# A hybrid decoder layer on one core: four small projection blocks moved from the first column tiles to the seventh, attention's units two ticks earlier, and one group's third weight sum made by accumulating transfers

## The chip, the cores and the metric

The kernel runs on one core of a Trainium2 chip. The metric is device time in microseconds (us) of one execution. TensorE (PE) multiplies; VectorE (DVE), ScalarE (ACT) and GpSimd (POOL) do the element-wise work; SP and POOL issue the DMAs that this change is about.

## The reference

One decoder layer over 512 tokens and 2048 columns, in fp32. `z = rms_norm(x) @ w_in` is cut by columns into q, k, v, an attention gate, and four parts of a convolution branch. Attention is causal over a window of 128 keys, with 16 query heads on 4 key heads, a norm and a partial rotation of q and k, and a learned sink. The convolution branch is `c_b * conv3(c_c * c_h)`, with three taps. Each branch is gated by a SiLU, and `x = x + concat(...) @ w_out`. Then

```
gate = sigmoid(rms_norm(x) @ w_ple_gate + b_ple_gate)
e    = rms_norm(p @ w_ple_proj)
x    = x + gate * e
```

where p is 512 x 256. The change touches where `p @ w_ple_proj` is computed, the timing of attention, and how a sum of weight blocks for `w_ple_gate` is made.

## The kernel before, in words

Every fp32 product is made of three matmuls on rounded halves: `halves` (L198) casts a tile to its high part on ACT (wh, L199) and subtracts on DVE for the low part (wl, L200). A matmul takes a 128 x 128 weight and 512 columns.

**The grouped products.** Most of the work is nine groups (five of `w_mid`, which are columns of w_in, two of `w_out`, two of `w_ple_gate`) of 28 steps, 12 matmuls each, in a scheme with seven products f = 1 to 7 over sums of weight blocks. `loads` and `load_more` (L144) bring blocks of 512 KB into the buffers wx, wy and ws; `sums` makes the sums of blocks in place. The third of them, for f = 7, is `tt(x, y, x, subtract)` on DVE (L191), four per group. For the groups in T3_BY_DMA that subtraction is left out, and L1368 to L1372 queue something else for each of the four blocks: `load_again` (L171) loads one block anew over the x block, and three steps later `add_block` (L166) adds another to it by an accumulating DMA that POOL issues. The first goes out after step 3 + 2i of the group (5 + 2i in the groups 5 and 7, which LATE lists), i counting the blocks. The order of PE is as written in the code in all parts; in the groups that of the other engines is too.

**The section before and the section here.** Group 0 runs first. Then (L670 on) comes the section that the change is about, where only PE's order is by hand and a scheduler orders the rest of the engines. It has seven column tiles of w_in, c_c and c_h of four convolution channels' tiles in turn, the last c_h behind the loop at L1383. `gemm_tile` (L702) makes a tile: 16 k, three matmuls each (L711), two weight blocks of 512 KB from a list `jobs`. `next_job` takes the next block of the list, splits the one after it, and `fetch` loads two further ahead into four raw buffers (L619). After each odd k it calls `tick`: eight ticks a tile, six matmuls apart. `at(when, fn)` hangs work on a tick. Attention and the preparation of k and q ride on these ticks:

- tick 4: `make_k(1)`, tick 6: `make_v`, tick 7: `make_k(0)`. `make_k` turns k on PE into a psm bank, of which there is one (ps_m), copies it to kr on ACT (L740), and makes khh and kll, high and low halves, by four more ACT casts (L745, L746) and four DVE subtractions (L747, L748).
- the norm and rotation of half of q (`square_q`, `rstd_q`, `rope_q`) at ticks 18 to 26.
- 16 units of attention `attention(j, n, when)`, with when = 13 + 35u // 15 for unit u: `turn_q` for every second unit at when − 4 (PE turns q into the same psm bank, L772; ACT and DVE make st, L776 and L777), `scores` at when (eight matmuls, L794 and L795, into two pss banks; the mask and row maximum on DVE, L800, into a prob buffer, of which there are two; exponentials on ACT, L807), `turn` at when + 5 (PE turns prob into pst, L822; halves give pth and ptl), `values` at when + 8 (into one pso bank, L832), and an accumulating DMA at when + 12.

**e's blocks.** `e_block(n)` (L854) makes one of four column blocks of p @ w_ple_proj for all 512 tokens: 24 matmuls (L874) into four banks, two pss and two pst, those that scores and turn use, each drained by a Square on ACT with its row sums (L865), a product by the gain on DVE (L867), and a DMA that POOL issues (L868). It takes one job of the list. `mids` says before which k of which tile an e block runs: block 0 at k = 8 of the first tile, blocks 1, 2, 3 at k = 0, 4, 8 of the second. The four w_ple_proj blocks stand among the first eight jobs.

**The first gate group** is group 7. Its gate values get their bias by accumulating DMAs on POOL (`add_b`, L1266), then a sigmoid (L1285), and a product with e (L1289).

Of the kernel before, what the change touches and what calls it, by code (L numbers as in the profile page):

```python
# [27 lines left out]
TQ, TK, TV, TGA, TCB, TCC, TCH, TGC = 0, 8, 10, 12, 20, 28, 36, 44  # L28
# [7 lines left out]
def hymba_layer(ctx: ExitStack, tc: tile.TileContext, io):  # L36
# [57 lines left out]
    NG = len(groups)  # L94
    chunks = [(0, 1, 2, 3)] * 5 + [(0, 1, 3, 2), (0, 1, 2, 3), (0, 1, 3, 2), (0, 1, 3, 2)]
    LATE = (5, 7)
    T1_BY_DMA, T3_BY_DMA = (0, *range(2, NG - 1)), (4, 5, 6)
    steps = []
    for g in range(NG):
        c0, c1, c2, c3 = chunks[g]  # L100
# [23 lines left out]
    for g in range(NG):  # L124
        w, n = groups[g]
# [72 lines left out]
    def halves(h, l, src):  # L198
        nc.scalar.copy(h, src)  # L199
        tt(l, src, f32(h), op=ALU.subtract)  # L200
# [259 lines left out]
    def flat(t):  # L460
        return t.rearrange("p a b -> p (a b)")
# [32 lines left out]
    for c in range(8):  # L494
# [20 lines left out]
        for i in range(2):  # L515
            k = 2 * c + i
# [47 lines left out]
    def head_sums(z, out, junk):  # L564

        sq = junk.rearrange("p (h d) -> p h d", d=HD)
        nc.scalar.activation(sq, z, AF.Square)
        nc.vector.tensor_reduce(out, sq, axis=mybir.AxisListType.X, op=ALU.add)

    def head_rstd(ms, eps):  # L570


        stt(ms, ms, 1.0 / HD, eps.unsqueeze(2).broadcast_to(ms.shape), op0=ALU.mult, op1=ALU.add)
        power(ms, ms)
# [8 lines left out]
    def q_of(t, n):  # L583
        return qs[t, n].rearrange("p b (h d) -> p b h d", d=HD)
# [3 lines left out]
    def square_q(t, n, b, junk):  # L588
        if b == 0:
            rq[t, n] = small.tile([P, 2, 8], F32, name="msq", bufs=4)  # L590
        head_sums(q_of(t, n)[:, b], rq[t, n][:, b], junk("sqq"))

    def rstd_q(t, n):
        blocks = slice(2 * t, 2 * t + 2)
        head_rstd(rq[t, n], eps_tok[:, blocks])

    def rope_q(t, n):
        rope(q_of(t, n), 0, slice(2 * t, 2 * t + 2), mtile)
# [5 lines left out]
    for j, s in enumerate((6, 6, 7, 7, 9, 9, 10, 10)):  # L604
        soon(after, s, form7, j)

    jobs = [io["w_in"][TCC, 0], io["w_ple_proj"][0], io["w_in"][TCC, 1], io["w_ple_proj"][1],
            io["w_in"][TCH, 0], io["w_ple_proj"][2], io["w_ple_proj"][3], io["w_in"][TCH, 1]]
    for i in range(1, 4):
        jobs += [io["w_in"][t + i, c] for t in (TCC, TCH) for c in range(2)]  # L610
    raws, splits, job = {}, {}, [0]

    def blocks_of(t):
# [68 lines left out]
    def mtile(name):  # L682
        return misc.tile([P, T], F32, tag="m", name=name)
# [5 lines left out]
    def at(when, fn):  # L689
        later.append((when, len(later), fn))  # L690
# [31 lines left out]
    for t in range(2):  # L722
        rope_q(t, 1)
        for b in range(2):
            at(18 + 2 * t + b, lambda t=t, b=b: square_q(t, 0, b, mtile))
        at(20 + 2 * t, lambda t=t: rstd_q(t, 0))
        at(24 + 2 * t, lambda t=t: rope_q(t, 0))
    mask = cw.tile([P, 2 * P], F32, name="mask", bufs=1)
    nc.gpsimd.dma_start(mask, io["mask"])
    vv = vvp.tile([P, NB, NKV, 2, HD], F32R, name="vv")  # L730
# [51 lines left out]
    def attention(j, n, when):  # L782

        lo = 0 if n else P
        cell = {}

        def scores():
            sc = [ps_s.tile([P, 2, 2 * P], F32, name="pss") for _ in range(2)]
            ks = slice(n * P + lo - P, (n + 1) * P)
            for r in range(4):  # L790
                i = 2 * (n % 2) + r // 2
                q = turned[j, n // 2, r % 2][:, i * P : (i + 1) * P]
                out = sc[r // 2][:, r % 2, lo:]
                nc.tensor.matmul(out, q, khh[j][:, ks], start=True, stop=False)  # L794
                nc.tensor.matmul(out, q, kll[j][:, ks], start=False, stop=True)  # L795
            t = ap.tile([P, 4, 2 * P], F32, name="prob")
            negm, sums, sk = (small.tile([P, 4], F32, name=x) for x in ("negm", "sums", "sk"))
            r_q = rq[n // 2, j // 2][:, n % 2, 4 * (j % 2) : 4 * (j % 2) + 4]
            for r in range(4):
                nc.vector.tensor_tensor_reduce(  # L800
                    t[:, r, lo:], sc[r // 2][:, r % 2, lo:], mask[:, lo:], HD**-0.5, NEG,
                    ALU.add, ALU.max, negm[:, r : r + 1],
                )
            tt(negm, negm, r_q, op=ALU.mult)
            stt(negm, negm, -1.0, nsink[:, 4 * j : 4 * j + 4], op0=ALU.mult, op1=ALU.min)
            for r in range(4):
                nc.scalar.activation(  # L807
                    t[:, r, lo:], t[:, r, lo:], AF.Exp, scale=r_q[:, r : r + 1], bias=negm[:, r : r + 1],
                    accum_out=sums[:, r : r + 1],
                )  # L810
            tt(sk, sink[:, 4 * j : 4 * j + 4], negm, op=ALU.add)
            nc.scalar.activation(sk, sk, AF.Exp)
            tt(sums, sums, sk, op=ALU.add)
            nc.vector.reciprocal(rs[:, n, 4 * j : 4 * j + 4], sums)
            cell["t"] = t

        def turn():
            cell["pt"] = []
            for kt in range(lo // P, 2):
                pt_ = ps_t.tile([P, T], F32, name="pst")  # L820
                for r in range(4):
                    nc.tensor.transpose(pt_[:, r * P : (r + 1) * P], cell["t"][:, r, kt * P : (kt + 1) * P], ident)  # L822
                h, l = (ap.tile([P, T], F32R, name=x) for x in ("pth", "ptl"))
                halves(h, l, pt_)
                cell["pt"].append((n - 1 + kt, h, l))

        def values():
            po = ps_o.tile([P, 4, P], F32, name="pso")
            pts = cell["pt"]
            for i, (b, h, l) in enumerate(pts):  # L830
                w = vv[:, b, j].rearrange("p s d -> p (s d)")
                nc.tensor.matmul(po, w, h, start=i == 0, stop=False)  # L832
                nc.tensor.matmul(po, w, l, start=False, stop=i == len(pts) - 1)
            up = mtile("up").rearrange("p (r t) -> p r t", t=P)
            nc.scalar.copy(up, po)
            rows = attn_dram[j].rearrange("(r d) (n t) -> d r n t", d=HD, n=NB)[:, :, n]
            nc.gpsimd.dma_start(rows, up[:HD])
            cell["add"] = lambda: nc.gpsimd.dma_start(rows, up[HD:], accum_op=ALU.add)

        if n % 2 == 0:  # L840
            at(when - 4, lambda: turn_q(j, n // 2))
        at(when, scores)
        at(when + 5, turn)
        at(when + 8, values)
        at(when + 12, lambda: cell["add"]())

# [7 lines left out]
    def e_block(n):  # L854

        pg = pgs[n]
        if n < 3:
            load_pg(n + 1)
        ws = next_job()
        banks = [flat(ps_s.tile([P, 2, 2 * P], F32, name="pss")) for _ in range(2)]  # L860
        banks += [ps_t.tile([P, T], F32, name="pst") for _ in range(2)]

        def take_e(t):
            e = mtile("e")
            nc.scalar.activation(e, banks[t], AF.Square, accum_out=esq[:, t, n : n + 1])  # L865
            e = mtile("e")
            tt(e, banks[t], pg, op=ALU.mult)  # L867
            nc.gpsimd.dma_start(e_dram[t // 2][n][:, t % 2], e)  # L868

        for t in range(NB):  # L870
            for k in range(2):
                h, l = (a[:, k, t * P : (t + 1) * P] for a in pts)
                for i, (a, w) in enumerate(((h, ws[0]), (l, ws[0]), (h, ws[1]))):
                    nc.tensor.matmul(banks[t], a, w[:, k], start=k == 0 and i == 0, stop=k == 1 and i == 2)  # L874
            for i in (t,):
                take_e(i)
# [1 line left out]
    load_pg(0)  # L878
    order = [(j, n) for j in (2, 3, 0, 1) for n in range(NB)]
    for u, (j, n) in enumerate(order):  # L880
        attention(j, n, 13 + 35 * u // 15)
    mids = {0: {8: lambda: e_block(0)}, 1: {k: lambda n=n: e_block(n) for n, k in ((1, 0), (2, 4), (3, 8))}}


    for i in range(4):
        ps = gemm_tile(ps_g.tile([P, T], F32, name="psg"), mids.get(2 * i))
        zc = mtile("zc") if i < 3 else rowp.tile([P, T], F32, tag="rows", name="zc")
        tt(zc, ps, rx2, op=ALU.mult)
        if i == 3:
            break  # L890
        ps = gemm_tile(ps_g.tile([P, T], F32, name="psg"), mids.get(2 * i + 1))
        u = cw.tile([P, T + HD], F32, name="u")
        nc.gpsimd.memset(u[:, 0:2], 0.0)
        tt(u[:, 2 : T + 2], ps, zc, op=ALU.mult)
        y = mtile("yconv")
        nc.scalar.activation(y, u[:, 0:T], AF.Copy, scale=convw[:, 0, i : i + 1])
        for s in (1, 2):
            stt(y, u[:, s : s + T], convw[:, s, i : i + 1], y, op0=ALU.mult, op1=ALU.add)
        nc.gpsimd.dma_start(conv_dram[i], y)
# [493 lines left out]
    u, y = itile("u"), rowp.tile([P, T], F32, tag="rows", name="yconv")  # L1393
# [121 lines left out]
```

## Time and profile before

| what | us |
|---|---|
| median of 3 runs | 919.99 (919.91 to 920.25) |
| the profiled execution | 919.36 |
| its span | 917.6 |
| outside the span | 1.76 |
| PE busy | 905.9 |
| DVE busy | 723.8 |
| ACT busy | 542.7 |
| POOL busy | 160.8 |

The profile is of one execution. Start times are us from the span's start; the busy time of an instruction overlaps its neighbours', so two instructions that follow at once start a little closer than the first one's duration. In brackets behind a row stands how long the engine was idle before it, and what ended that. "X <- Y" in the list of waits reads: this instruction of X, waiting for that tile written by Y, in us in total, how many times, and the longest one. In a group of transfers the last number is the median time from issue to landing. A psum bank is named by its tile: psg the gemm's, psm, pss, pst, pso as above, psp the groups'.

### The profile page before, as it was taken

The page shows a single profiled execution, that of the slowest core. Times are in us where ns is not written, and L with a number is a line of the kernel's source. Part 1 is how long each engine was busy: PE and PEld are TensorE (multiplying, and loading weights), DVE is VectorE, ACT ScalarE, POOL GpSimd, SP SyncE. Part 2 cuts the span into 40 slices and gives each one's busy share as a digit, 9 for nine tenths or more (in the row PEclk, how much of TensorE's full clock was granted, in tenths as well). Part 3 has the DMA queues.
Part 4 walks back from the last instruction along what each step waited for, and adds up shares of the span by engine and source line. Part 5 has one row for each costly group of instructions (what it writes and reads, how often), then busy time and mean ns, then how long its engine had stood idle before and what let it go on. Part 6 is the DMA issues. An engine that isn't in the chain of part 4 may idle for free.

```text
span 917.6 us, 12067 instructions
## 1 busy us (share of the span) xinstructions
PE 905.9 (99%) x4178; PEld 751.4 (82%) x4178; DVE 723.8 (79%) x1063; ACT 542.7 (59%) x878; POOL 160.8 (18%) x211
## 2 busy tenths in 40 slices
PE   9999999999999999999999999999999999999997
PEld 8888888878888888888888888888888888887885
DVE  6878888788765777877768678987858887889678
ACT  6767847778863443454345357766556666555453
POOL 4232132143230001100120110102120111001100
PEclk9999999999999999999999999999999999999999
DMA  9999558434469767558578887858996993588647
GB/s 315 362 292 308 197 63 309 162 81 108 93 116 313 269 204 234 159 169 233 157 185 240 239 222 233 253 141 229 341 291 193 211 295 92 139 248 267 183 138 218
DMA packets 71389, 195.06 MB, mean 213 GB/s; under 512 B 8355, under 2 KB 14819, under 8 KB 71328
## 3 DMA queue, kind: packets, MB, share of 16 engines
q1 hardware_dynamic: 48096, 132.14, 42.3%
q0 software_dynamic: 23088, 62.15, 30.5%
q8 instruction: 32, 0.52, 0.2%
q14 instruction: 29, 0.24, 0.1%
q10 hardware_dynamic: 144, 0.01, 0.0%
HBM read 162.81 MB, written 31.46 MB: 212 GB/s over the span
## 4 chain that ended last, share of the span: by engine, by line
PE 89%; DVE 6%; ACT 3%; issue 2%; DVEq 0%; ACTq 0%
PE psp L241 67%; PE psg L711 6%; PE psp L519 5%; PE pst L241 4%; PE pst L993 2%; ACT prob L807 1%; PE pss L874 1%; PE pst L1391 1%; PE pst L874 1%; PE pst L822 1%; DVE wl L200 1%; DVE z L1289 1%; DVE prob L800 1%; DVE ptl L200 1%; PE pso L832 1%
## 5 line engine op out<-in xcount | busy, mean ns | idle before, releaser
L241 PE MATMUL psp<-wh,form 128*128 128x512 f32 x1280 | 395.3, 390 | 0.0
L241 PEld LDWEIGHTS psp<-wh,form 128*128 128x128 f32 x1280 | 239.4, 188 | 49.2
L241 PE MATMUL psp<-wl,form 128*128 128x512 f32 x640 | 249.5, 390 | 1.3 <-DVE wl L200 1.2
L200 DVE TENSOR_TENSOR wl<-wy,wh 128x1024 fp32r<-128x1024 f32 x108 | 131.5, 1222 | 60.3 <-ACT wh L199 59.7
L199 ACT CAST wh<-wy 128x1024 fp32r<-128x1024 f32 x108 | 113.4, 1051 | 90.2 <-PE psp L241 70.6
L241 PEld LDWEIGHTS psp<-wl,form 128*128 128x128 f32 x640 | 120.1, 188 | 27.4 <-DVE wl L200 2.5
L200 DVE TENSOR_TENSOR wl<-wx,wh 128x1024 fp32r<-128x1024 f32 x72 | 88.0, 1223 | 50.0 <-ACT wh L199 49.8
L199 ACT CAST wh<-ws 128x1024 fp32r<-128x1024 f32 x72 | 75.9, 1054 | 74.5 <-PE psp L241 53.8
L199 ACT CAST wh<-wx 128x1024 fp32r<-128x1024 f32 x72 | 75.6, 1052 | 74.3 <-PE psp L241 52.7
L241 PE MATMUL psp<-wh,hsh 128*128 128x512 f32 x304 | 118.6, 390 | 0.0
L241 PE MATMUL psp<-wl,hsh 128*128 128x512 f32 x304 | 118.3, 389 | 0.0
L241 PE MATMUL psp<-wh,hsl 128*128 128x512 f32 x304 | 118.3, 389 | 0.0
L200 DVE TENSOR_TENSOR wl<-ws,wh 128x1024 fp32r<-128x1024 f32 x72 | 88.1, 1223 | 27.1 <-ACT wh L199 26.8
L189 DVE TENSOR_TENSOR wy<-wy,ws 128x1024 f32<-128x1024 f32 x72 | 87.7, 1218 | 0.0
L241 PEld LDWEIGHTS psp<-wh,hsh 128*128 128x128 f32 x304 | 57.1, 188 | 11.8
L241 PEld LDWEIGHTS psp<-wh,hsl 128*128 128x128 f32 x304 | 57.1, 188 | 11.8
L241 PEld LDWEIGHTS psp<-wl,hsh 128*128 128x128 f32 x304 | 57.1, 188 | 11.8
L711 PE MATMUL psg<-hsh,wh 128*128 128x512 f32 x112 | 45.2, 403 | 0.0
L711 PE MATMUL psg<-hsh,wl 128*128 128x512 f32 x112 | 43.8, 391 | 0.0
L711 PE MATMUL psg<-hsl,wh 128*128 128x512 f32 x112 | 43.8, 391 | 0.0
L199 ACT CAST wh<-raw 128x1024 fp32r<-128x1024 f32 (+1 forms) x29 | 29.2, 1006 | 22.5 <-DMA raw<-in_w_ple_proj 7.7
L200 DVE TENSOR_TENSOR wl<-raw,wh 128x1024 fp32r<-128x1024 f32 (+1 forms) x29 | 33.8, 1165 | 9.5 <-ACT wh L199 9.2
(218 smaller groups left out, 1307.1 us busy)
## 6 DMA issues: line engine op xcount, KB each, us to landing
ws<-in_w_mid SPq DMA_DIRECT2D x40, 512.0 KB, 4.5
wx<-in_w_mid SPq DMA_DIRECT2D x24, 512.0 KB, 4.2
wy<-in_w_mid SPq DMA_DIRECT2D x20, 512.0 KB, 7.6
h<-form POOLq DMA_DIRECT2D x32, 256.0 KB, 5.8
wy<-in_w_mid POOLq DMA_DIRECT2D x16, 512.0 KB, 8.1
raw<-in_w_in SPq DMA_DIRECT2D x16, 512.0 KB, 4.1
wx<-in_w_out SPq DMA_DIRECT2D x16, 512.0 KB, 7.6
ws<-in_w_out SPq DMA_DIRECT2D x16, 512.0 KB, 5.6
```

Source lines behind the costliest of these rows:

```text
L189: tt(y, y, got[g, "s1" if f == 6 else "s0", c], op=ALU.add)
L199: nc.scalar.copy(h, src)
L200: tt(l, src, f32(h), op=ALU.subtract)
L241: nc.tensor.matmul(ps[t], a, w[:, i], start=start and first and i == 0 and n == 0, stop=last and i == 1 and n == 2, skip_group_check=not s ...
L519: nc.tensor.matmul(kv_ps[t // 2][:, t % 2], hs[k][a][:, t * P : (t + 1) * P], kv_split[c][w][:, i], start=k == 0 and n == 0, stop=k == KT ...
L711: nc.tensor.matmul(ps, w[:, k % 8], a, start=k == 0 and n == 0, stop=k == KT - 1 and n == 2)
L800: nc.vector.tensor_tensor_reduce(t[:, r, lo:], sc[r // 2][:, r % 2, lo:], mask[:, lo:], HD**-0.5, NEG, ALU.add, ALU.max, negm[:, r : r + 1],)
L807: nc.scalar.activation(t[:, r, lo:], t[:, r, lo:], AF.Exp, scale=r_q[:, r : r + 1], bias=negm[:, r : r + 1], accum_out=sums[:, r : r + 1],)
L822: nc.tensor.transpose(pt_[:, r * P : (r + 1) * P], cell["t"][:, r, kt * P : (kt + 1) * P], ident)
L832: nc.tensor.matmul(po, w, h, start=i == 0, stop=False)
L874: nc.tensor.matmul(banks[t], a, w[:, k], start=k == 0 and i == 0, stop=k == 1 and i == 2)
L993: nc.tensor.transpose(pt[:, b], quads[b // 2][:, b % 2, f * P : (f + 1) * P], ident)
```

## The change

Three things are done.

1. The list of jobs holds the sixteen blocks of w_in in the order of the tiles, with the four blocks of w_ple_proj from the fourteenth place on (one before the seventh tile's second w_in block and three behind it). The e blocks 0, 1, 2 run at k = 8, 10 and 12 of the seventh tile, block 3 behind that tile and its product by rx2.
2. Attention's when is 11 + 35u // 15, so all units run two ticks earlier, and the first turn_q falls on tick 7. The turn comes at when + 6. The norm and rotation of q are three ticks earlier.
3. Group 7 is added to T3_BY_DMA: four DVE subtractions go, and four loads on SP and four accumulating DMAs on POOL, of 512 KB each, come in after the steps 5, 7, 9, 11 and three steps later.

```diff
-    T1_BY_DMA, T3_BY_DMA = (0, *range(2, NG - 1)), (4, 5, 6)
+    T1_BY_DMA, T3_BY_DMA = (0, *range(2, NG - 1)), (4, 5, 6, 7)
...
-    jobs = [io["w_in"][TCC, 0], io["w_ple_proj"][0], io["w_in"][TCC, 1], io["w_ple_proj"][1],
-            io["w_in"][TCH, 0], io["w_ple_proj"][2], io["w_ple_proj"][3], io["w_in"][TCH, 1]]
-    for i in range(1, 4):
-        jobs += [io["w_in"][t + i, c] for t in (TCC, TCH) for c in range(2)]
+    jobs = [io["w_in"][t + i, c] for i in range(4) for t in (TCC, TCH) for c in range(2)]
+    jobs[13:14] = [io["w_ple_proj"][0], jobs[13]] + [io["w_ple_proj"][i] for i in range(1, 4)]
...
-            at(18 + 2 * t + b, lambda t=t, b=b: square_q(t, 0, b, mtile))
-        at(20 + 2 * t, lambda t=t: rstd_q(t, 0))
-        at(24 + 2 * t, lambda t=t: rope_q(t, 0))
+            at(15 + 2 * t + b, lambda t=t, b=b: square_q(t, 0, b, mtile))
+        at(17 + 2 * t, lambda t=t: rstd_q(t, 0))
+        at(21 + 2 * t, lambda t=t: rope_q(t, 0))
...
-        at(when + 5, turn)
+        at(when + 6, turn)
...
-        attention(j, n, 13 + 35 * u // 15)
-    mids = {0: {8: lambda: e_block(0)}, 1: {k: lambda n=n: e_block(n) for n, k in ((1, 0), (2, 4), (3, 8))}}
+        attention(j, n, 11 + 35 * u // 15)
+    mids = {6: {k: lambda n=n: e_block(n) for n, k in ((0, 8), (1, 10), (2, 12))}}
...
         if i == 3:
+            e_block(3)
             break
```

The lines behind L610 stand two lower in the changed kernel, and the last ones one.

## The prediction

> **What bounds the kernel now.** I read the page first: the engines' busy time, and the chain that ended last.
>
> ```profile
> span 917.6 us, 12067 instructions
> PE 905.9 (99%) x4178; PEld 751.4 (82%) x4178; DVE 723.8 (79%) x1063; ACT 542.7 (59%) x878; POOL 160.8 (18%) x211
> ```
>
> TensorE (PE) works in 905.9 of 917.6 us. None of the edits adds or removes a matmul (4178 before, and none of the moved blocks changes its product), so the time can only move by what PE waits: 917.6 − 905.9 = 11.7 us. Second came PE's waits by releaser, third the windows, which say where the idle time lies (columns: the window, its length, then busy time of PE, PE's weight loads, DVE, ACT and POOL, the granted clock, the DMA share, GB/s).
>
> ```profile
> PE pst L822 <- DVE ptl L200: 2.4, 3, 1.5
> PE psp L241 <- DVE wl L200: 1.2, 1, 1.2
> PE pst L368 <- DVE zeros L364: 1.1, 1, 1.1
> PE pst L822 <- DVE negm L804: 0.6, 1, 0.6
> 126.00:150.00 24.00, 24.00 (x111) 19.89 (x110) 20.04 (x42) 15.95 (x30) 2.21 (x4) 1.00 0.79 219
> 165.50:274.00 108.50, 105.38 (x590) 89.14 (x589) 84.11 (x291) 84.24 (x222) 34.71 (x39) 1.00 0.47 107
> 274.00:286.00 12.00, 12.00 (x55) 9.93 (x54) 2.55 (x3) 2.91 (x4) 2.06 (x3) 1.00 0.87 253
> 817.00:828.00 11.00, 9.74 (x42) 7.43 (x41) 9.73 (x11) 7.44 (x9) 1.70 (x2) 1.00 0.81 234
> 905.00:917.60 12.60, 6.50 (x29) 5.07 (x27) 8.63 (x15) 2.25 (x5) 0.00 (x0) 0.88 0.80 261
> ```
>
> The change can reach two of these. In attention (165.5 to 274) PE idles 108.5 − 105.38 = 3.12 us. In the first gate group (817 to 828) it idles 11 − 9.74 = 1.26 us. The start (1.1) and the tail (6.1) are untouched. So the change can gain at most 3.12 + 1.26 = 4.4 us. The stretch from 126 to 150, where two e blocks stand now, has no wait at all: whatever goes wrong there is new time.
>
> The profiled execution took 919.36 us (917.6 of span, 1.76 around it), 0.63 below the median of 919.99. The sum is made against 919.36, and 0.63 is added at the end. The bound of 0.2%, about what a measurement of this kernel can tell from no change, is 1.84 us.
>
> **First part: e's blocks leave the first two column tiles.** The chain of waits gives PE's own order where they stand:
>
> ```profile
> 126.34 5.45 PE psg L711 x24
> 131.78 0.44 PE psm L739 x4
> 132.22 2.75 PE pss L874 x12
> 134.98 2.72 PE pst L874 x12
> 137.70 4.08 PE psg L711 x18
> 141.78 0.44 PE psm L739 x4
> ```
>
> Between the two L739 groups (the transposes of make_k(1) and make_k(0), at ticks 4 and 7) lie an e block, 2.75 + 2.72 = 5.47 us, and three ticks of the gemm, 4.08 us. The e block goes, the three ticks stay. Both groups write the one psm bank, so the second must wait until ScalarE (ACT) has read the first into kr. Now ACT's timeline (start, duration, and in brackets the idle time ahead and what ended it), with two transfers by time to landing ahead of it and one row of DVE behind it, used further down:
>
> ```profile
> rows_r<-rx_tok POOLq DMA_DIRECT2D x1, 2.0 KB, 11.3
> mask<-in_mask POOLq DMA_DIRECT2D x1, 128.0 KB, 12.8
> 127.10 1.02 ACT L320 ACTIVATE z<-psp 128x1024 f32<-128x1024 f32 x1
> 135.80 1.05 ACT L199 CAST wh<-raw 128x1024 fp32r<-128x1024 f32 x1 [7.67 <-DMA raw<-in_w_ple_proj]
> 136.75 0.68 ACT L740 ACTIVATE kr<-psm,kq 128x512 f32<-128x512 f32 x1
> 137.47 0.62 ACT L745 CAST khh<-kr 64x512 fp32r<-64x512 f32 x1
> 139.92 0.59 ACT L865 ACTIVATE e<-pss 128x512 f32<-128x512 f32 x1
> 163.90 0.69 DVE L867 TENSOR_TENSOR e<-pss,pg 128x512 f32<-128x512 f32 x1 [0.61 <-ACT e L865]
> ```
>
> ACT's first kr was ready to run at 132.2 and ran at 136.75: the cast of the fourth weight block stands ahead of it and waits 7.67 us for its transfer. 2 KB took 11.3 us to land and the mask's 128 KB 12.8 at that time, so I put the lateness down to those small writes, which the change does not touch, and take the fourth block to land then again, though it is now one of w_in. Before, the e block covered this. The changed order on ACT, from that cast on (kr and khh are k turned and its rounded half, st the turned q; L738, L743, L744 and L774 are L740, L745, L746 and L776 of before):
>
> ```order
> L199 CAST wh_1540<-raw_1418 128x1024
> L738 ACTIVATE kr_1448<-psm_1449,kq_220 128x512
> L743 CAST khh_1455<-kr_1448 64x512
> L744 CAST khh_1455<-kr_1448 64x512
> L743 CAST khh_1461<-kr_1448 64x512
> L744 CAST khh_1461<-kr_1448 64x512
> L738 ACTIVATE kr_1499<-psm_1500,kq_220 128x512
> L743 CAST khh_1506<-kr_1499 64x512
> L744 CAST khh_1506<-kr_1499 64x512
> L743 CAST khh_1512<-kr_1499 64x512
> L744 CAST khh_1512<-kr_1499 64x512
> L774 CAST st_1523<-psm_1518 64x512
> ```
>
> The cast still stands ahead of the first kr, and the second kr behind four khh. Next PE's order at tick 7, first before, then changed (psm is the bank in dispute, L737 and L770 are L739 and L772 of before):
>
> ```order
> L711 MATMUL psg_1417<-hsh_548,wl_1472 128x512
> L739 MATMUL psm_1556<-ident_208,kv_710 128x128
> L739 MATMUL psm_1556<-ident_208,kv_711 128x128
> L739 MATMUL psm_1556<-ident_208,kv_712 128x128
> L739 MATMUL psm_1556<-ident_208,kv_713 128x128
> L711 MATMUL psg_1417<-hsh_615,wh_1471 128x512
> L711 MATMUL psg_1417<-hsl_616,wh_1471 128x512
> ```
>
> ```order
> L709 MATMUL psg_1417<-hsh_548,wl_1421 128x512
> L737 MATMUL psm_1500<-ident_208,kv_710 128x128
> L737 MATMUL psm_1500<-ident_208,kv_711 128x128
> L737 MATMUL psm_1500<-ident_208,kv_712 128x128
> L737 MATMUL psm_1500<-ident_208,kv_713 128x128
> L770 MATMUL psm_1518<-ident_208,z_1047 128x128 x4
> L709 MATMUL psg_1417<-hsh_615,wh_1420 128x512
> ```
>
> With attention two ticks earlier, the first turn_q (11 − 4 = tick 7) now follows make_k(0) at once, in the same bank; before, two ticks and an e block stood between. On PE's clock: 126.34 + 5.45 + 0.44 + 4.08 = 136.3 for make_k(0). Its bank comes free when kr(1) ends, 136.75 + 0.68 = 137.4: 1.1 us of wait. Transposes to 137.9. Then turn_q needs kr(0), which ACT reaches after the four khh, at 139.92 (where its next instruction starts in the trace), and ends at 140.6: 2.7 us more. **New wait: 3.8 us**, all on PE, with the whole gemm queued behind. It would be less only if the block landed earlier: with kr(1) at 132.2 it would be about 0.9 (third rival).
>
> At the other end, three e blocks go into the seventh tile and one behind it. Each is 5.4 us of PE against four times a Square on ACT and a product on DVE (0.59 and 0.69 by the last two rows above), which hides them; behind it the window 274 to 286 has room, DVE being busy 2.55 of 12 us. I take +0.2 for the banks that the last convolution shares with them; at most the whole last block's drain, four products, 2.7 us, and not below 0.
>
> **Second part: attention's units.** A unit's scores are summed against the mask on DVE, into the prob buffer, of which there are two, so this step of unit u+2 waits for the turn of u, and the scores of u+3 wait for the banks that it empties.
>
> ```profile
> 184.06 0.41 DVE L800 CUSTOM_DVE_ANT_0 prob<-pss,mask 128x256 f32<-128x256 f32 x1
> 185.09 0.42 DVE L800 CUSTOM_DVE_ANT_0 prob<-pss,mask 128x256 f32<-128x256 f32 x1
> 187.60 1.16 PE L822 MATMUL pst<-ident,prob 128*128 128x128 f32 x8 [1.45 <-DVE ptl L200]
> 188.04 1.22 DVE L200 TENSOR_TENSOR wl<-raw,wh 128x1024 fp32r<-128x1024 f32 x1
> ```
>
> The four take 185.09 + 0.42 − 184.06 = 1.45 us. The turn moves from +5 to +6 and the scores of u+3 come at +7: two ticks lay between, now one, 4.08 / 3 = 1.36 us. That is just short of 1.45 when DVE is free, and short by more when a weight block's split (1.22) or a q half stands ahead on DVE. Stepping the sixteen units through by these durations gives waits of 0.45 (scores of the first unit, whose st comes late after tick 7), 0.8 (its values), 0.9, 0.35, 1.0 and 1.15 (scores of the fourth, fifth, seventh and tenth), 0.47 (values of the eighth): 5.1 us. The later turn, for its part, gives DVE's ptl a tick more, which was the 2.4 of before. Against 3.12 before, this is **+2.0**. Bounds: −3.1, if every wait goes, and +3.4, if the largest old wait, 1.45, stays beside the new ones: 5.1 + 1.45 − 3.12.
>
> **Third part: the gate group.** Four DVE subtractions (L191, 1.22 us each) become four loads on SP and four accumulating transfers on POOL.
>
> ```profile
> 807.72 0.86 POOL L1266 DMA_DIRECT2D z<-in_b_ple_gate  x1 [25.16 <-DVE wl L200]
> 816.24 1.06 ACT L1285 ACTIVATE z<-z 128x1024 f32<-128x1024 f32 x1 [2.33 <-DMA z<-in_b_ple_gate]
> 818.27 1.23 DVE L200 TENSOR_TENSOR wl<-wy,wh 128x1024 fp32r<-128x1024 f32 x1 [2.36 <-ACT wh L199]
> 827.34 0.50 PE L241 MATMUL psp<-wl,form 128*128 128x512 f32 x1 [1.19 <-DVE wl L200]
> z<-in_b_ple_gate POOLq DMA_DIRECT2D x3, 512.0 KB, 8.5
> 645.90 1.19 POOL L1179 DMA_DIRECT2D x<-in_x_tok  x1 [4.87 <-issue]
> 641.83 5.00 SPq L158 DMA_DIRECT2D wx<-in_w_out  x3
> 801.67 0.33 SPq L158 DMA_DIRECT2D wx<-in_w_ple_gate  x1
> 610.00:817.00 207.00, 207.00 (x946) 171.98 (x945) 167.15 (x210) 128.05 (x188) 29.48 (x34) 1.00 0.78 219
> ```
>
> The wait of 1.2 is a chain: the third bias add is issued late on POOL (807.72), lands 8.5 us later, so the sigmoid at 816.24 holds ACT, so the splits are late, and PE waits at 827.34. POOL's order there, before and then changed (z is the gate's tile, wx the weight sum):
>
> ```order
> L1244 TENSOR_SCALAR nr_x2_7166<-r_x2_7164 128x4
> L1266 DMA z_7259<-in_b_ple_gate 128x1024
> L1266 DMA z_7233<-in_b_ple_gate 128x1024
> L1266 DMA z_7408<-in_b_ple_gate 128x1024
> L1292 DMA z_7408<-x201_3133 128x1024
> ```
>
> ```order
> L1243 TENSOR_SCALAR nr_x2_7166<-r_x2_7164 128x4
> L169 DMA wx_6710<-in_w_ple_gate 128x1024
> L169 DMA wx_6729<-in_w_ple_gate 128x1024
> L169 DMA wx_6756<-in_w_ple_gate 128x1024
> L1265 DMA z_7261<-in_b_ple_gate 128x1024
> L169 DMA wx_6779<-in_w_ple_gate 128x1024
> L1265 DMA z_7234<-in_b_ple_gate 128x1024
> L1265 DMA z_7414<-in_b_ple_gate 128x1024
> ```
>
> Group 5 already has this form, and PE has no wait from 610 on, through its end. The next group's first wx load starts at 641.83 there and at 801.67 in the gate group, so the same place lies 159.8 us later. Its third add on POOL went out at 645.90, which becomes 805.7, some 1.9 us ahead of 807.72. ACT's wait of 2.33 shrinks by that to 0.4, so I take PE's 1.2 as gone: **−1.2**, between −1.26 and +1.0 (the fourth weight sum now queues between two bias adds on POOL; one place there costs 0.86).
>
> **The sum.** 3.8 + 0.2 + 2.0 − 1.2 = +4.8: 919.36 + 4.8 = 924.2 profiled, and 924.2 + 0.63 = 924.8 as a median.
>
> **The rivals.**
> *No change* (0.14): the 3.8 stays, but attention's waits all go, and the gate's. 3.8 − 3.1 − 1.2 = −0.5, so 919.5. For it: each wait of attention was on a step the change gives more time. Against: one tick is shorter than the four reductions.
> *Faster* (0.12): the fourth block lands before about 132, or ACT runs kr(1) first, so tick 7 costs 0.9 instead of 3.8, and attention's waits go: 0.9 − 3.1 − 1.2 = −3.4, 916.6. It decides on when that cast ends: every us before 136.3 up to the turn is gained. Against it stand the 11.3 and 12.8 us to landing.
> *The clock gate* (0.10): PE rests nearly 3.8 us with 0.44 of work inside. In the trace the clock falls only where PE stands still for long:
>
> ```profile
> 914.00:917.60 3.60, 0.00 (x0) 0.00 (x0) 0.56 (x2) 0.00 (x0) 0.00 (x0) 0.59 0.24 81
> ```
>
> It is 1.00 through the attention window with its wait of 1.45 us, and 0.59 here with PE idle for 3.6 us. If it fell to 0.59 for such a stretch after tick 7, 3.6 × 0.41 = 1.5 us would be lost, up to twice that: +6.3 to +7.8, 926.3 to 927.8. The Trainium skill, TensorE: Matmul & The Clock Gate, section Part 1: The HAM clock gate (the "warmup" mystery), has the clock halve after an idle window of about 3.4 us on a free-running counter; by that page the estimate is 1.7 us more, and the row agrees that a still PE loses clock. The rest of the sum does not need it. Since the 0.44 of transposes splits the pause into 1.1 and 2.7, I hold it unlikely.
> *Crowding at the end* (0.09): e's writes, 16 of them, meet the loads for group 1. The e blocks leave their bank drains in front of the last convolution, and PE waits the 2.7 of the bound above: 924.8 + 2.5 = 927.3.
> The forecast itself has 0.55, between 922 and 927. Slower: 0.55 + 0.10 + 0.09 = 0.74; same 0.14; faster 0.12. The range takes the no-change case in from 919.4 and the two worse ones up to 928.6, leaving the faster case and little else.
>
> **What would show it.** In the changed profile: two PE waits near 136 to 141, on L737 for kr and on L770 for kr, 1.1 and 2.7; ACT's cast of the fourth block starting near 135.8 after a wait for a DMA; scores' waits on L792 for the reduction L798 (L794 and L800 of before); no wait of psp for wl near 827 (4 us later); PE busy still about 906. I am wrong if the window around tick 7 has no idle PE, or if attention's idle time falls under 1 us.

## The result and the profile after

| | median us | range | runs |
|---|---|---|---|
| before | 919.95 | 919.68 to 920.25 | 4 |
| changed | 925.12 | 924.81 to 926.82 | 4 |

The ratio is 1.0062 (95% interval 1.0049 to 1.0075): slower by 0.5 to 0.75%, clear of the 0.2% that can be told here. 924.8 was forecast as the median, and 924.2 for the profiled execution. That one is the longest of the four, 926.82 us with a span of 925.0; the other three have spans of 922.9 to 923.2, so a rerun's profile is read beside it below.

The changed kernel's page and its list of PE's waits:

```profile
span 925.0 us, 12059 instructions
PE 910.6 (98%) x4178; PEld 753.7 (81%) x4178; DVE 719.9 (78%) x1059; ACT 543.7 (59%) x878; POOL 164.6 (18%) x215
```
```profile
PE psm L770 <- ACT kr L738: 2.6, 1, 2.6
PE pss L792 <- DVE negm L798: 1.7, 3, 0.7
PE pso L831 <- DVE ptl L200: 1.3, 2, 0.7
PE psm L737 <- ACT kr L738: 1.1, 1, 1.1
PE pst L1390 <- DVE e L865: 0.2, 1, 0.2
```

The two waits for kr stand where they were expected, 1.1 and 2.6. The waits for ptl and negm at the turn are gone, and the wait of psp for wl with them; new are three waits of scores for the reduction (1.7) and two of values for ptl (1.3). PE is idle for 925.0 − 910.6 = 14.4 us, 2.7 more than before. But PE is also busy for 4.7 us more, with the same 4178 matmuls: it ran slower somewhere. The windows show where (columns as before; the granted clock is the third number from the end):

```profile
136.00:139.00 3.00, 1.11 (x7) 0.45 (x5) 2.06 (x3) 2.92 (x5) 0.00 (x0) 1.00 1.03 236
139.00:140.00 1.00, 0.00 (x0) 0.00 (x0) 0.99 (x2) 0.97 (x2) 0.00 (x0) 0.92 1.02 412
140.00:146.00 6.00, 5.19 (x15) 4.22 (x16) 5.38 (x9) 5.56 (x10) 0.00 (x0) 0.50 0.42 171
146.00:147.00 1.00, 1.00 (x4) 0.82 (x3) 0.97 (x2) 0.92 (x2) 0.00 (x0) 0.67 0.00 0
165.50:254.00 88.50, 85.48 (x473) 70.88 (x472) 66.71 (x238) 68.78 (x187) 27.80 (x33) 1.00 0.49 106
```

From 139.8 (0.92 in the second row) to 146.7 (0.67 in the fourth), 6.8 us that begin within the pause, the granted clock is one half: the clock gate, which had 1 chance in 10. The last row is attention's long stretch, with 3.0 us of idle PE. Now PE and ACT around tick 7, from their timelines:

```profile
137.52 0.66 PE L737 MATMUL psm<-ident,kv 128*128 128x128 f32 x4 [1.06 <-ACT kr L738]
140.81 1.12 PE L770 MATMUL psm<-ident,z 128*128 128x128 f32 x4 [2.63 <-ACT kr L738]
143.01 0.63 PE L709 MATMUL psg<-hsh,wh 128*128 128x512 f32 x1
```
```profile
135.84 1.05 ACT L199 CAST wh<-raw 128x1024 fp32r<-128x1024 f32 x1 [7.59 <-DMA raw<-in_w_in]
136.79 0.68 ACT L738 ACTIVATE kr<-psm,kq 128x512 f32<-128x512 f32 x1
140.07 0.69 ACT L738 ACTIVATE kr<-psm,kq 128x512 f32<-128x512 f32 x1
```

ACT waits 7.59 us for the fourth block, as it did before, and both kr come behind it; a gemm matmul at half the clock takes 0.63 by its row instead of 0.39, and the next starts 0.43 later instead of 0.23.

For the rest one length is used, from the start of the section's first gemm matmul to the start of the last matmul of the last convolution. Its two ends, before and after:

```profile
126.17 0.39 PE L711 MATMUL psg<-hsh,wh 128*128 128x512 f32 x1
284.77 0.39 PE L1391 MATMUL pst<-hsh,wl 128*128 128x512 f32 x1
```
```profile
126.30 0.39 PE L709 MATMUL psg<-hsh,wh 128*128 128x512 f32 x1
293.91 0.39 PE L1390 MATMUL pst<-hsh,wl 128*128 128x512 f32 x1
```

The section took 158.6 before and 167.6 after, 9.0 more; the whole span grew 7.4, so the groups gave back 1.6 to 1.7. The section's 9.0 are 3.7 of waits at tick 7, 2.8 of half-speed matmuls (twelve of the gemm, each followed about 0.2 too late, and the four transposes ahead of them), and 2.5 that no single row carries.

### The profile page after: what moved, and what is told of

Same layout as the page of the kernel before. It is cut to its first block, busy times and chain, and to the rows that moved or that the text cites. A ratio compares the mean times of both kernels' runs of the same rounds, so it can differ in the third digit from the quotient of the medians.

```text
span 925.0 us, 12059 instructions
## 1 busy us (share of the span) xinstructions
PE 910.6 (98%) x4178; PEld 753.7 (81%) x4178; DVE 719.9 (78%) x1059; ACT 543.7 (59%) x878; POOL 164.6 (18%) x215
## 4 chain that ended last, share of the span: by engine, by line
PE 68%; DVE 2%; ACT 1%; issue 1%; DVEq 0%; ACTq 0%
PE psp L241 59%; PE pst L241 4%; PE pst L992 2%; PE pst L1390 1%; PE pss L872 1%; PE pst L872 1%; PE psg L709 1%; DVE z L1288 1%; DVE wl L200 1%; DVE wy L189 0%; ACT z L998 0%; ACT z L1111 0%; DVE form L200 0%; ACT wh L199 0%; PE pso L831 0%
## 5 line engine op out<-in xcount | busy, mean ns | idle before, releaser
L805 ACT ACTIVATE prob<-prob,negm,msq 128x256 f32<-128x256 f32 (+1 forms) x64 | 36.0, 565 | 15.7 <-DVE negm L803 15.6
```

The costliest lines, as they stand in the source:

```text
L805: nc.scalar.activation(t[:, r, lo:], t[:, r, lo:], AF.Exp, scale=r_q[:, r : r + 1], bias=negm[:, r : r + 1], accum_out=sums[:, r : r + 1],)
```

## The experiments

Twelve kernels, measured against three sets of runs of the kernel before (919.42, 919.61 and 919.82 us). "Section" is the length just defined, in the kernel's profile. After these profiles two theories were open. **The pair theory**: the loss is the two waits at tick 7 and the clock that they cost, while attention's own balance is about nothing. **The prediction's sum**: tick 7 costs 3.8, and attention's new order 2.0 on top.

| kernel | median us | against before (95%) | section |
|---|---|---|---|
| before | 919.42 to 919.82 | | 158.6 |
| changed, again | 924.93 | 1.0063 (1.0051, 1.0076) | 165.6 |
| gate group only | 917.59 | 0.9981 (0.9972, 0.9989) | 158.6 |
| attention's old ticks | 919.57 | 1.0002 (0.9993, 1.0010) | 160.6 |
| early make_k | 922.33 | 1.0030 (1.0018, 1.0041) | 162.7 |
| eleven more matmuls | 924.87 | 1.0058 (1.0044, 1.0072) | 165.6 |
| early make_k, turn +5 | 920.22 | 1.0004 (0.9996, 1.0013) | 160.8 |
| early make_k, start 13 | 918.37 | 0.9986 (0.9978, 0.9995) | 158.9 |
| before with turn +6 | 919.87 | 1.0004 (0.9996, 1.0013) | 158.8 |
| early make_k, early q | 922.96 | 1.0035 (1.0023, 1.0048) | 163.9 |
| early make_k, start 13, q at 18 | 918.82 | 0.9990 (0.9982, 0.9999) | 159.6 |
| early make_k, start 13, later e | 923.22 | 1.0033 (1.0020, 1.0046) | 161.1 |
| without the small writes | 922.28 | 1.0027 (1.0017, 1.0037) | 163.3 |

**The gate group's part alone.** The kernel before, with

```diff
-    T1_BY_DMA, T3_BY_DMA = (0, *range(2, NG - 1)), (4, 5, 6)
+    T1_BY_DMA, T3_BY_DMA = (0, *range(2, NG - 1)), (4, 5, 6, 7)
```

> The kernel before with only the third part of the change (group 7's third sum by accumulating transfers). Both theories (the loss lies at tick 7, or in attention) say the same of it: the PE wait of 1.2 us for wl at 827 goes, nothing else moves, so about 918.7, a gain of 1.2 us (0.13%). Rival: the four extra transfers of 512 KB delay other loads of the group, and a new wait takes the place of the old one: 919.9 or more.

Measured 917.59, 1.83 under before; the profile has no wait of psp for wl, and the span is 916.0, 1.6 less. The part gains, and more than the 1.2 of the wait. PE's rows at that place, the kernel before first, tell why:

```profile
825.54 0.61 PE L241 MATMUL psp<-wh,form 128*128 128x512 f32 x2
827.34 0.50 PE L241 MATMUL psp<-wl,form 128*128 128x512 f32 x1 [1.19 <-DVE wl L200]
```
```profile
825.28 0.62 PE L241 MATMUL psp<-wh,form 128*128 128x512 f32 x2
825.73 0.39 PE L241 MATMUL psp<-wl,form 128*128 128x512 f32 x1
```

A wait is counted from the end of the matmul before, 0.39 behind its start, but matmuls that aren't held up start 0.23 apart. From the start of the pair at 825.54 to that of the next matmul pass 1.80 us, where the second kernel takes 0.45: 1.35 lost, not 1.19. The matmul behind it, at 827.68, comes another 0.11 late, and at 823.14, where the list has no wait, 0.23 and 0.11 are lost the same way. That is 1.8 in all, the whole gain. So the lists of waits count too little, by about 0.16 for each wait, and leave small delays out; lengths from start to start don't.

**Attention's ticks as before.** The changed kernel with start 13, turn +5 and q at 18, 20, 24:

```diff
-        attention(j, n, 11 + 35 * u // 15)
+        attention(j, n, 13 + 35 * u // 15)
...
-        at(when + 6, turn)
+        at(when + 5, turn)
```

> The changed kernel with attention's times as before (start at tick 13, turn at +5, the preparation of q at 18): the first turn_q falls on tick 9, two ticks behind make_k(0), while the e blocks stay in the seventh tile. If the loss comes from the pair in one bank at tick 7: the wait of make_k(0) for kr stays (1.1 us), the turn_q's of 2.6 shrinks to at most 0.2, the clock stays at 1.00, and the time is 919.95 + 1.1 - 1.2 + 0.2 = about 920.0. If the moved e blocks as such cost the time (their end, their weights' transfers), it stays near 924.5.

919.57, near the first case's 920.0, but by another sum. The wait of make_k(0) was 0.2 here, not 1.1, since the block landed about a us earlier; yet the section is 2.0 longer than before, and the gate group's 1.8 makes up for it. The moved e blocks as such do not cost the 5 us.

**Early make_k.** The changed kernel, with k's turns ahead of the late cast in ACT's queue:

```diff
-    at(4, lambda: make_k(1))
+    at(1, lambda: make_k(1))
...
-    at(7, lambda: make_k(0))
+    at(3, lambda: make_k(0))
```

> The changed kernel with make_k(1) at tick 1 and make_k(0) at tick 3 (4 and 7 in the change), so that ACT has both kr and their eight khh ahead of the cast that waits for the fourth weight block. If the loss is the two waits at tick 7 (3.7 us) and the clock that they take (1 to 2.8 us): no PE wait of psm, the clock 1.00 from 136 to 150, about 919.8 (919.0 to 920.6), no difference from the kernel before. If 2 us of the loss lie in attention's new order, as the prediction's sum had it: 921.2.

922.33, which neither number hits. The waits at tick 7 are gone and the clock is 1.00, yet 2.9 over before remain, and with the gate group's gain the section is 4.1 longer than before. The pair theory, in which attention costs nothing, falls. The list of waits of this kernel:

```profile
PE pss L792 <- DVE negm L798: 3.1, 5, 1.0
PE pso L831 <- DVE ptl L200: 1.3, 2, 0.7
```

Scores wait for the reduction five times, 3.1 in all, where the changed kernel has 1.7: with PE not held up at tick 7, attention waits more. The two waits that are new are those of the third and fourth unit (0.41 and 1.01).

**Eleven more matmuls in the pause.** The changed kernel, with PE kept busy through the long wait:

```diff
     def turn_q(j, t):
-
+        if not turned:
+            po = ps_o.tile([P, 4, P], F32, name="pso")
+            for _ in range(11):
+                nc.tensor.matmul(flat(po), pts[0][:, 0, :P], pts[0][:, 0], start=True, stop=True)
```

> The changed kernel with eleven more matmuls (11 x 0.227 = 2.5 us), of no use to the result, into an idle bank between make_k(0) and the first turn_q, so that PE works through the pause of 2.6 us instead of standing still; the wait itself stays. If the still PE costs clock on top of the wait: granted clock 1.00 from 136 to 150 and about 923.3, that is 1 to 2.8 us faster than the changed kernel, with more work. If the clock plays no part in the median: 925.1, or up to 0.5 more where the eleven outlast the wait.

The clock stays at 1.00, and the time doesn't fall: 924.87, against 924.93 for the changed kernel (below). Where the clock's part went is seen in two windows of three kernels, the changed kernel again first, this one second, early make_k last:

```profile
136.00:150.00 14.00, 11.17 (x52) 8.90 (x51) 12.84 (x28) 10.44 (x18) 0.64 (x1) 0.88 0.51 177
150.00:165.50 15.50, 14.82 (x79) 12.02 (x78) 11.72 (x37) 12.00 (x32) 2.97 (x3) 1.00 0.12 42
```
```profile
136.00:150.00 14.00, 13.24 (x67) 10.64 (x66) 13.00 (x28) 10.41 (x19) 1.93 (x1) 1.00 0.48 174
150.00:165.50 15.50, 13.89 (x75) 11.21 (x74) 11.72 (x38) 11.99 (x33) 1.68 (x3) 1.00 0.15 49
```
```profile
136.00:150.00 14.00, 14.00 (x75) 11.96 (x74) 11.97 (x30) 7.39 (x17) 2.90 (x1) 1.00 0.48 168
150.00:165.50 15.50, 13.38 (x73) 10.28 (x72) 13.32 (x46) 12.04 (x30) 1.59 (x4) 1.00 0.20 63
```

Between 150 and 165.5 PE is idle 0.7 us in the first, 1.6 in the second and 2.1 in the third. What PE loses before attention's first units, ACT and DVE use to get on, and PE waits less for them there. The first scores of the fourth unit, in the changed kernel and in this one:

```profile
161.50 0.38 PE L792 MATMUL pss<-khh,st 128*128 128x256 f32 x1
161.26 0.39 PE L795 MATMUL pss<-khh,st 128*128 128x256 f32 x1 [0.93 <-DVE negm L801]
```

The sections start at 126.39 and 126.13, so both have come this far in 35.1 us, with the half clock and without; in this kernel PE stands 0.93 instead. So the half clock of the rerun costs next to nothing: PE would have stood waiting. With early make_k the same scores come at 158.21, 32.2 after the section's start at 126.06. From there to the section's end all three kernels take 130.5 us: what is paid back is paid back within the first units. In the first profile nothing was. There these scores come 37.1 us after the section's start, 2.0 behind the rerun, by the 0.9 that kr came later and the 1.1 that the half clock took more.

**The changed kernel again.**

> The changed kernel once more, on one chip with the three that follow. About 1.0056 of the kernel before (5.2 us over it, near 924.7 where that takes 919.5), and a mean granted clock of 0.994 to 0.997 in every execution, against 0.998 to 1.000 of before. If the clock plays no part, 0.998 to 1.000 here too.

924.93, and mean clocks of 0.996 to 0.998 against 0.998 to 1.000 of before (with one of 0.996). Two of the six executions have 0.998, which can't be told from before. The stretch at half clock is shorter here, 3.4 us from about 141.1 to 144.5. It costs 1.7: from 140.04 to 144.65 PE starts four transposes and eleven gemm matmuls, 2.9 us of work at full clock. The first profile's was 6.8, and its time 1.6 to 2.0 us above its three companions'. That the one causes the other is shown only as far as the 1.1 us above: the rerun's own longest execution, 927.62, has a mean clock of 0.997 like its companions.

**What in attention costs: the turn or the start.** Three kernels. Early make_k with the turn back:

```diff
-        at(when + 6, turn)
+        at(when + 5, turn)
```

> The changed kernel with early make_k (ticks 1 and 3), and the turn back at +5. If the turn at +6 is what costs attention its 2 to 3 us (one tick between it and the scores that need the buffer): the waits of scores for the reduction go, the old waits of the turn for ptl come back (about 3), and the section takes as long as before: 1.8 us under the kernel before by the gate group's part, plus up to 0.4, near 918.0. If the cost is the start at tick 11, it stays 2.9 over, near 922.3.

Early make_k with the old start:

```diff
-        attention(j, n, 11 + 35 * u // 15)
+        attention(j, n, 13 + 35 * u // 15)
```

> The changed kernel with early make_k, the turn at +6, but the units started at tick 13 as before. If the turn at +6 costs: 922.3, as with the start at 11. If the start at 11 costs: near 918.0.

The kernel before with the later turn:

```diff
-        at(when + 5, turn)
+        at(when + 6, turn)
```

> The kernel before with only the turn moved from +5 to +6. If that is what costs attention: 2 to 4 us slower, 921.5 to 923.5, with waits of scores (L794) for the reduction (L800). If the later turn gives DVE the tick that it lacked, as the change may be read: the 2.4 us of waits for ptl go, 917.5. If neither: 919.5.

920.22, 918.37 and 919.87. The old start takes 3.96 us off early make_k, with the turn still at +6; the old turn takes 2.1 off, with the start still at 11; and in the old kernel the later turn costs nothing that can be told (+0.26). So the later turn is harmless at a start of 13, where it even goes with the second-best time of all, and costs 1.9 of the section at a start of 11. With the start at 11 the section is 2.2 longer than before already at +5; how much of that is the start's alone stays open, since early make_k with both old ticks was not run. In the old kernel both cases of the expectation came half true:

```profile
PE pss L794 <- DVE negm L800: 1.8, 2, 1.1
```

The turn's waits for ptl and negm, 3.0 in all, are gone, and scores wait 1.8 in their place. Attention's waits in the version with the old start, and its long window:

```profile
PE pss L792 <- DVE negm L798: 1.3, 2, 0.7
PE pst L820 <- DVE e L865: 1.0, 1, 1.0
```
```profile
165.50:254.00 88.50, 87.80 (x483) 74.50 (x482) 65.41 (x224) 70.33 (x189) 28.06 (x36) 1.00 0.52 114
```

Scores wait twice instead of five times, and in the long window PE is idle 0.7 us, where the changed kernel has 3.0 and the kernel before 3.1; the 1.0 for an e block comes behind that window. For the fourth unit's scores both traces can be laid side by side. DVE and PE with the start at 11:

```profile
156.00 0.68 DVE L775 TENSOR_TENSOR st<-psm,st 64x512 fp32r<-64x512 f32 x1 [0.23 <-ACT st L774]
156.71 0.75 DVE L897 SCALAR_TENSOR_TENSOR yconv<-u,conv_w,yconv 128x512 f32<-128x512 f32 x1
157.38 0.42 DVE L798 CUSTOM_DVE_ANT_0 prob<-pss,mask 128x256 f32<-128x256 f32 x1
```
```profile
155.20 0.60 PE L820 MATMUL pst<-ident,prob 128*128 128x128 f32 x4
158.21 0.39 PE L792 MATMUL pss<-khh,st 128*128 128x256 f32 x1 [1.01 <-DVE negm L798]
```

The turn of the first unit frees the prob buffer at about 155.6, and then a half of q (0.68) and a tap of the convolution (0.75), which comes at the end of every second tile, stand ahead of the reduction on DVE. With the start at 13 the same scores come two ticks later against the tile, the tap has run before the turn, and the wait is 0.68. This is one wait followed to its rows. Of the seven of early make_k (4.4 us) three fall on the first four units (2.1), the others on the 7th, 10th, 14th and 15th.

**The preparation of q as the cause.** Early make_k with q's preparation ahead of the units (9, 11, 15):

```diff
-            at(15 + 2 * t + b, lambda t=t, b=b: square_q(t, 0, b, mtile))
-        at(17 + 2 * t, lambda t=t: rstd_q(t, 0))
-        at(21 + 2 * t, lambda t=t: rope_q(t, 0))
+            at(9 + 2 * t + b, lambda t=t, b=b: square_q(t, 0, b, mtile))
+        at(11 + 2 * t, lambda t=t: rstd_q(t, 0))
+        at(15 + 2 * t, lambda t=t: rope_q(t, 0))
```

> The changed kernel with early make_k (922.3 by the run above), start at 11 and turn at +6 as changed, but the preparation of q (square, rstd, rope) at ticks 9, 11, 15 instead of 15, 17, 21, ahead of most units. If the first units wait because DVE and ACT do the preparation of q among them: 919 to 920. If the start at 11 costs by something else (the first units' own chain, or the splits of weight blocks): 922.3.

And the version with the old start, with q's preparation where it was before, at 18, 20 and 24 in the same three lines:

> The version with early make_k and the start at 13 (918.37 by the run above), with the preparation of q where it was before, at 18, 20, 24 instead of 15, 17, 21. If that preparation among the units is what makes them wait: 920 or more. If not: 918.4.

922.96 and 918.82. Neither differs from the kernel it was made from by more than the intervals allow (1.0035 to 1.0030, 0.9990 to 0.9986), and neither reaches what the cause would have given (919 to 920, and 920 or more). The preparation of q is not the cause.

**The e blocks later still.** The version with the old start has one wait of 1.0 us of a turn for an e block's drain. Two blocks are put behind the tile:

```diff
-    mids = {6: {k: lambda n=n: e_block(n) for n, k in ((0, 8), (1, 10), (2, 12))}}
+    mids = {6: {k: lambda n=n: e_block(n) for n, k in ((0, 12), (1, 14))}}
...
         if i == 3:
+            e_block(2)
             e_block(3)
```

with the four w_ple_proj blocks behind the tile's second w_in block in the list.

> The version with early make_k and the start at 13 (918.37), with the e blocks at k = 12 and 14 of the seventh tile and two behind it, so that the last turn no longer waits 1.0 us for an e block's drain. If that wait is on the path: 917.4. If it only moves to the last convolution's bank: 918.4.

923.22, worse than both cases. Its waits:

```profile
PE pst L1391 <- DVE e L865: 3.0, 1, 3.0
PE psp L241 <- DVE wl L200: 1.2, 1, 1.2
```

The drain of the last block is now bare: 3.0, where 2.7 was the bound for it. And the gate group's wait of 1.2 is back, though the group is made as in the changed kernel. Two transfers landed late there, by POOL's and ACT's rows:

```profile
803.75 0.86 POOL L169 DMA_DIRECT2D wx<-in_w_ple_gate  x1 [8.81 <-DMA wx<-in_w_ple_gate]
810.90 1.05 ACT L199 CAST wh<-wx 128x1024 fp32r<-128x1024 f32 x1 [3.13 <-DMA wx<-in_w_ple_gate]
819.05 1.06 ACT L1285 ACTIVATE z<-z 128x1024 f32<-128x1024 f32 x1 [2.33 <-DMA z<-in_b_ple_gate]
```

The fourth weight sum waited 8.81 for its own reload, 6.11 in the version with the old start, and landed late. The third bias add went out no later against its group (35.3 us behind POOL's r_x in both kernels), but at 808.37, before that sum had landed, and the sigmoid behind it waits 2.33 as in the kernel before. So the gate group's gain, 1.8 us, hangs on when these transfers land. That the late reload delays the bias add is likely by this order, and not shown apart.

**Why the fourth block is late.** The changed kernel without the write of the 512 factors:

```diff
-    soon(after, 23, lambda: nc.gpsimd.dma_start(r_dram.rearrange("b p -> p b"), rx2_tok))
...
-    nc.sync.dma_start(rx2, r_dram.rearrange("(o b) p -> o (b p)", o=1).broadcast_to([P, T]))
+    nc.sync.dma_start(rx2, io["ple_norm_gain"][:, :T])
```

> The changed kernel without the write of 512 factors of 4 bytes to memory (rows_r), the rows that are read back from it being read from another array, so that the convolution is scaled by the wrong numbers. If those small writes hold the fourth weight block: its cast on ACT ends before 132, PE waits 0 for kr at the first psm group and 0.7 at the turn_q instead of 0.2 to 1.1 and 2.6, and the time is near 922.3, as with early make_k. If the lateness has another cause: 924.9.

It held but for 0.2 us at the cast's end (132.2) and 0.1 at the turn_q. The mask's transfer and ACT's cast, and PE's wait at tick 7, in this kernel:

```profile
mask<-in_mask POOLq DMA_DIRECT2D x1, 128.0 KB, 2.4
```
```profile
131.16 1.05 ACT L199 CAST wh<-raw 128x1024 fp32r<-128x1024 f32 x1 [3.46 <-PE psg L709]
```
```profile
PE psm L770 <- ACT kr L738: 0.8, 1, 0.8
```

The mask lands in 2.4 us instead of 12.8, the cast waits for PE instead of a transfer, and of the pair 0.8 is left (0.7 expected). 922.28 is the time of early make_k, reached from the other side. The two weight blocks that are issued beside the write, the fourth and the one behind it, landed so in the changed kernel and in this one:

```profile
DMA to landing us min/median/max: 12.8/13.2/13.6
DMA to landing us min/median/max: 3.7/3.8/4.0
```

The edit also lets the rows be read sooner, but that read isn't what held the blocks: in the changed kernel it goes out at 131.55, when they had been out since 122.11 and 124.37.

**The best version** is the gate group's part alone, 917.59. It beats the kernel before by 0.19% (0.11 to 0.28%) and the changed one by 7.3 us.

## Why the prediction was right, and where its sum was not

The median came out within 0.3 us, and so did the sign, but part of that is luck: the pair was taken too dear, the clock was left out of the sum, and the gate group gains more than was taken. By the rerun's section the account is 2.8 for the pair, 1.7 for the half clock, 2.5 for attention and the end, less 1.8 for the gate group, 5.2 in all; the forecast was 3.8 + 0 + 2.2 − 1.2 = 4.8. The profiled execution, forecast at 924.2, took 926.82, with 2.8 of half clock in it.

- **The pair at tick 7, 3.8.** The mechanism was right in each step: the late cast, kr behind it, the second kr behind four khh, one bank. Measured 1.06 + 2.63 = 3.69 in the first profile and 0.20 + 2.63 in the rerun, where the block came a us sooner. Undoing it (early make_k) gave 2.6 us, less than the pair and the half clock together. That the small writes hold the block was put down to two landing times, and is now shown.
- **Attention, +2.0.** The size came out in the changed kernel: 9.0 − 3.7 − 2.8 leaves 2.5 for attention and the end, and the rerun 7.0 − 2.8 − 1.7, the same, where 2.2 was forecast. The way to it was not as forecast. By the list attention waits 3.0, no more than before, not 5.1: three of the five waits stand where the stepping put them (values of the first unit, scores of the 7th and 10th), at 0.5 to 0.7 instead of 0.8 to 1.15, and scores of the 14th and values of the 15th weren't forecast. (Without the pair the scores of the fourth wait too, 1.01 for 0.9.) The rest lies in matmuls that start 0.1 to 0.2 late, which the list leaves out. Among them are values, for which the later turn leaves two ticks instead of three: near 246 they start 0.33 to 0.36 apart, not 0.23. And the reason given, "two ticks lay between, now one", doesn't hold for the later turn by itself: alone it costs +0.26. With the start at 11 it costs 1.9.
- **The two terms do not add.** Without the pair, attention and the end cost 4.1 (0.2 of it the end's), not 2.5: a pause of PE ahead of a stage that waits for ACT and DVE is partly paid back there. The sum added them as if each were on the path alone.
- **The gate group, −1.2.** Right in kind: the third bias add went out at 814.72, which less the 9.16 by which the group starts later (POOL's r_x at 779.42, before 770.26) is 805.6, against 805.7 forecast. ACT's wait for it is 0.20, where 0.4 was forecast. Measured −1.83; the surplus of 0.6 is what the list of waits leaves out.
- **The end, +0.2.** Measured 0.20 by the list of waits, so the crowding there, a rival with 0.09, did not come; the bound of 2.7 was met only with two blocks behind the tile (3.0).
- **The clock gate** was a rival with 0.10, on the ground that the 0.44 of transposes splits the pause. It happened in both profiles of the changed kernel, and by the mean clock (0.994 to 0.997) in eight of its ten executions, so PE was not "busy still about 906" but 910.6 in the first profile. The clock then is 0.50; the 0.59 that the price was worked out with is the mean of a window in which it changed. The half clock took 1.7 us in the rerun and 2.8 in the first profile, inside the price of 1.5 to 3, but in the median it can't be added: without it, in the kernel with eleven more matmuls, the time is the same. The Trainium skill, TensorE: Matmul & The Clock Gate, section Part 1: The HAM clock gate (the "warmup" mystery), gives a free-running window of about 3.4 us. The rerun's stretch at half clock, 141.1 to 144.5, agrees, and the first profile's is twice that; the idle time that set it off, 2.63 us in the rerun, is shorter than the page's rule asks.
- **Faster and no change** did not happen; the first hung on an early fourth block, which only the kernel without the small writes has, and even there 922.3 remain, so its sum of 916.6 was wrong too.

Left open: which of DVE's instructions make up the 3.9 that attention costs without the pair (one wait was followed to its rows, not all), and how much the start at 11 costs by itself.

## What to carry to other kernels

A block of PE work is also cover: before moving it, list what on the other engines finishes beneath it, and whose buffers they hold. When a change shifts a stage against a periodic one (units against tiles here), test the shift and the order within the stage separately, since one may be harmless alone and dear beside the other. Costs ahead of a stage that waits for another engine do not simply add to that stage's own waits. And compare lengths from start to start: a list of waits leaves small delays out.

## What the runs showed of the hardware

One transfer of 2 KB in pieces of 4 bytes kept three others from landing: the mask's 128 KB took 12.8 us beside it and 2.4 without, and two weight blocks of 512 KB 12.8 and 13.6 us instead of 3.7 and 4.0. The clock went by windows, not by the length of one wait. In each trace its changes lie whole multiples of 3.41 us apart (in the rerun 136.5, 3.4 and 774.8 us). On that grid, the windows that ended where the clock fell, in the first profile and the rerun, and two of the kernel with the later e blocks, across its wait of 3.0 us:

```profile
136.42:139.84 3.42, 0.69 (x5) 0.42 (x4) 2.88 (x4) 3.31 (x6) 0.00 (x0) 1.00 1.02 267
137.69:141.10 3.41, 1.06 (x7) 0.97 (x8) 2.87 (x5) 3.28 (x6) 0.00 (x0) 1.00 1.01 401
```
```profile
271.55:274.96 3.41, 2.15 (x10) 1.46 (x8) 0.73 (x2) 0.22 (x2) 2.44 (x5) 1.00 1.02 281
274.96:278.37 3.41, 1.62 (x7) 1.35 (x8) 2.13 (x3) 2.21 (x5) 0.54 (x1) 1.00 0.80 321
```

PE was busy 0.69 and 1.06 us in the first two, and the clock fell, in the rerun 1.06 us after PE had gone on. It was busy 2.15 and 1.62 in the others, the longer wait being spread over both, and the clock stayed at 1.00; four further executions of that kernel have mean clocks of 0.994 to 0.997, so there it seems to have fallen. So the same pause may cost the clock or not, by where it lies on the grid. No run was made to test this.
